# A fixed TensorE order for the projections of a hybrid DeltaNet and sparse-attention layer: chunk steps, transposes, projections and modulation interleaved

## The chip, the cores and the metric

The kernel runs on one core of a Trainium2 chip, in one launch. The metric is the device time of one execution in microseconds; a lower number is better. The kernel before took 3890.76 us (median of 3 runs, 3890.46 to 3893.05).

## What is computed

One inference step of one decoder layer, for a prompt of 2048 tokens (width 1024) and for 8 sampled tokens. Cut to what matters here:

```python
sh1, sc1, ga1, sh2, sc2, ga2 = split(silu(c) @ w_ada + b_ada, 6)       # modulation: 9 rows of c, w_ada is 1024 x 6144
h = rmsnorm(x, g_norm1) * (1 + sc1) + sh1
qkv, z, beta, a, aq, ak, av, iq, ik, iw = split(h @ w_in)               # w_in is 1024 x 3664
gq, gk, gv = silu(causal_conv4(qkv))                                   # then q and k are l2-normed
o_gdn = delta_rule_chunked(gq, gk, gv, decay, sigmoid(beta), s0)        # per chunk: (I + lower)^-1, then a state step
o_att = sparse_attn(rope(aq), rope(ak), av, rope(iq), rope(ik), iw)     # indexer picks 256 keys, then softmax
x = x + ga1 * (concat(rmsnorm(o_gdn) * silu(z), o_att) @ w_out)
h2 = rmsnorm(x, g_norm2) * (1 + sc2) + sh2
x = x + ga2 * ((silu(gate) * up) @ w_ffn_out)                           # gate, up = split(h2 @ w_ffn_in)
```

The outputs are the normed y of both, the new keys, values and index keys, the last rows before the convolution, and the new DeltaNet states.

## The kernel before

All matrix products keep fp32 precision. A large one is made of three matmuls (`mm3`, L157 to L162): operands are split into a high and a low part of the faster fp32r type, and high x high, high x low and low x high are added up in the same PSUM bank. So one product of a 128x128 block with 512 columns is three matmuls of 128x512, on lines L160, L161 and L162 of the profile.

The work is in two phases. Phase 1 (`phase1`) handles the prompt in four groups of 512 tokens; phase 2 does the attention of blocks 4 to 15 (128 queries each), the sampled rows, the output projection and the FFN.

**Phase 1** begins with the modulation. Parts 0 and 1 (shift and scale of the first norm) use the raw fp32 w_ada, which lies in borrowed buffers (L321); parts 2 to 5 are spread over the groups and go through `weights` like any other weight: load (L143), ScalarE cast to the high part (L144), VectorE subtraction for the low part (L145), and two matmuls per 128 rows against the split conditioning `cTs` (L176, L177).

For each group, `project(g)` norms the rows of x (ScalarE squares, VectorE scaling), transposes them on TensorE into hh and hl (8 x 4 transposes, L372), multiplies the 80 narrow columns (wsh, wsl), and then goes through seven column tiles of 512: three that feed the convolution, and z, aq, kv and iq. Each tile is 8 k steps x 12 matmuls into four PSUM banks ("d"); a group is 672 of them. Group 0 casts and splits w_in and stores the result in DRAM ("kept", L148); groups 1 to 3 load it back in 512 KB pieces (wi<-kept, L138, three buffers). `conv` (L637 to L652) evacuates a convolution tile (ScalarE L642, VectorE L646, L648, L651) and stores it in DRAM (cT_d). `narrow` makes decay and beta on 128x16 tiles (VectorE, L551 to L597). `tok` rotates aq, ak and iq (VectorE, L632 to L635) and transposes them (L676, L686, L722).

`chunks(g)` then runs the DeltaNet of the group: four chunks of 128 tokens, in two pairs. The two `chunk` generators of a pair alternate: load the chunk from cT_d (L814), transpose q, k, v (L829), norm them (VectorE L845, L847, L852), transpose again, decay matrix (L868 to L876), products k·k and q·k (L882). `inverse` inverts both chunks' four heads at once, as 8 dependent steps of 32 matmuls of 32x32 in four levels (E·D, L763; copy by ScalarE, L765; D part, L770; E part, L774; each followed by a VectorE copy under a mask, L771 and L775), and four larger steps (L781 to L804). `state` multiplies by the state, makes the new one and the chunk's output (L916 to L948). The inverse and the transposes use two PSUM banks ("g"), `state` and attention two ("s").

**What sets the order.** The scheduler of the language orders every engine's instructions from the program's order, priorities and its own estimate of time. On TensorE it puts whatever it believes ready in front: projection matmuls of group g+1 between chunk steps of group g, and also FFN matmuls of phase 2. An engine executes its list in that order.

Of the kernel before, what the change touches and what calls it, by code (L numbers as in the profile page):

```python
# [56 lines left out]
S2, S4, LATE = 8, 1044, 8000  # L57

# [51 lines left out]

class K:
    def __init__(self, tc, A, O, dbg=None, ngroups=NG, stages=9):
        self.tc, self.nc, self.A, self.O = tc, tc.nc, A, O
        self.dbg = dbg or {}
        self.ng = ngroups
        self.stages = stages
        self.biases, self.kept = {}, {}

# [39 lines left out]
    def mm3(self, out, wh, wl, xh, xl, start, stop, **kw):  # L158
        nc = self.nc
        nc.tensor.matmul(out, wh, xh, start=start, stop=False, **kw)  # L160
        nc.tensor.matmul(out, wh, xl, start=False, stop=False, **kw)  # L161
        nc.tensor.matmul(out, wl, xh, start=False, stop=stop, **kw)  # L162
# [10 lines left out]
    def mm_s(self, out, s, wh, wl, start, stop):  # L173

        n = s.shape[1]
        self.nc.tensor.matmul(out[:n], s, wh, start=start, stop=False)  # L176
        self.nc.tensor.matmul(out[:n], s, wl, start=False, stop=stop)  # L177
# [95 lines left out]
    def modulation(self):  # L273
# [26 lines left out]
        for k in range(KB):  # L300
            nc.tensor.transpose(pc[:, k * 9:k * 9 + 9], sc[:9, k * 128:(k + 1) * 128], self.id[:9, :9])
        self.cT = cp.tile([128, KB, 9], F32, name="cT")
        nc.scalar.activation(self.cT, pc[:, :72].rearrange("p (k n) -> p k n", k=KB), AF.Copy, scale=0.5)
        pt = self.ps.tile([128, 512], F32, name="d", tag="d", bufs=4)
        nc.tensor.transpose(pt[:, :113], vec[:113], self.id[:113, :113])
        nc.vector.tensor_copy(self.cv, pt[:, :113])
        self.cTs = self.stack(cp, self.cT, KB, 9, "cTs")
# [3 lines left out]
    def modulate(self, part):  # L311

        nc, A, p, wp = self.nc, self.A, self.p, self.wp
        for hf in range(2):
            c0 = part * 1024 + hf * 512
            b0 = part * 8 + hf * 4
            pm = self.ps.tile([128, 512], F32, name="d", tag="d", bufs=4)
            n = 9 if part < 2 else 42
            for k in range(KB):
                if part < 2:  # L320
                    nc.tensor.matmul(pm[:9], self.cT[:, k, :], self.ada[part][k][:, hf * 512:hf * 512 + 512], start=k == 0, stop=k == KB - 1)  # L321
# [3 lines left out]
            m9 = self.m("m9")[:n, :512]  # L325
            nc.scalar.copy(m9, pm[:n])
            pt = self.ps.tile([128, 512], F32, name="d", tag="d", bufs=4)
            for m in range(4):
                nc.tensor.transpose(pt[:, m * n:m * n + n], m9[:, m * 128:(m + 1) * 128], self.id[:n, :n])
            pv = pt[:, :4 * n].rearrange("p (m n) -> p m n", m=4)  # L330
            mod = self.mod[:, b0:b0 + 4, :]
            nc.vector.tensor_tensor(mod, pv[:, :, 0:9], self.cv[:, 16 + b0:20 + b0].unsqueeze(2).to_broadcast([128, 4, 9]), op=OP.add)
            if part >= 2:
                nc.vector.tensor_tensor(mod, mod, pv[:, :, 32:41], op=OP.add)
# [27 lines left out]
    def norm_T(self, xt, ms, Amul, Badd, hh, hl, ptag, pbufs):  # L362

        nc, nblk, xn = self.nc, 4, xt
        for t in range(0, nblk, 2):
            r = self.rnorm(ms[:, t:t + 2])
            for a in range(2):
                nc.vector.tensor_scalar(xn[:, t + a, :], xt[:, t + a, :], r[:, a:a + 1], None, op0=OP.mult)
        for k in range(KB):
            pt = self.ps.tile([128, 512], F32, name=ptag, tag=ptag, bufs=pbufs)  # L370
            for t in range(nblk):
                nc.tensor.transpose(pt[:, t * 128:(t + 1) * 128], xn[:, t, k * 128:(k + 1) * 128], self.id)  # L372
            h = self.p.tile([128, 512], F32, name="ca", tag="ca", bufs=2)
            nc.vector.tensor_scalar(h, pt, Amul[:, k, 0:1], Badd[:, k, 0:1], op0=OP.mult, op1=OP.add)
            nc.scalar.copy(hh[:, k, :], h)
            nc.vector.tensor_tensor(hl[:, k, :], h, hh[:, k, :].bitcast(F32), op=OP.subtract)

    def norm_T_s(self, pool, xs, ms, Amul, Badd, ptag, pbufs):
# [4 lines left out]
        for k in range(KB):  # L383
            nc.tensor.transpose(pt[:, k * NS:(k + 1) * NS], xn[:, k * 128:(k + 1) * 128], self.id[:NS, :NS])
# [6 lines left out]
    def phase1(self, es):  # L391
# [35 lines left out]
        self.modulate(0)  # L427
        self.modulate(1)
# [10 lines left out]
        self.ends()  # L439
# [22 lines left out]
    def project(self, g):  # L462
# [3 lines left out]
        xt = self.load_x(g) if g else self.x0  # L466
        hh = p.tile([128, KB, GT], F32R, name="hh", bufs=1)
        hl = p.tile([128, KB, GT], F32R, name="hl", bufs=1)
        ms = self.msq()
        for t in range(4):  # L470
            self.squares(ms[:, t], xt[:, t, :])
        self.norm_T(xt, ms, self.A1, B1, hh, hl, "d", 4)
        if samp:
# [3 lines left out]
            hs = self.norm_T_s(self.p1, xs, ms[:NS, 4:5], self.A1, B1, "d", 4)  # L477
# [3 lines left out]


        pd = self.ps.tile([128, 512], F32, name="d", tag="d", bufs=4)
        for k in range(KB):
# [1109 lines left out]
```

## Time and profile before

| | before |
|---|---|
| median of 3 runs | 3890.76 us (3890.46 to 3893.05) |
| profiled execution | 3895.36 us |
| its span | 3893.4 us |
| mean granted TensorE clock | 0.939 |
| TensorE / VectorE / ScalarE / GpSimd busy | 91% / 55% / 39% / 17% |
| idle before L774, behind VectorE's masked copy (54 to 1538 us) | 17.9 us in 16 waits |
| idle before L176, behind ScalarE's cast (54 to 1538 us) | 14.7 us in 20 waits |

A row of a timeline has the start, the length of the last record or of the group, the engine, the line, the operation, output and inputs, their shapes, the number of records, and in brackets the idle time before it with what ended that. fp32 matmuls leave two records each, fp32r matmuls one. In rows of windows the columns are the stretch, its length, the busy time of TensorE, its weight loads, VectorE, ScalarE and GpSimd with the number of instructions, then the granted TensorE clock (1.00 is full speed), the busy share of the DMA engines, and GB/s. A row of waits has the engine and line that waited, what it waited for, the total in us, how often, and the longest.

### The profile page before, as it was taken

How to read it: one execution, taken by the hardware profiler on the slowest of the kernel's cores; microseconds unless marked ns; L12 is line 12 of the kernel's file. 1: busy time of each engine (PE TensorE's matmuls, PEld its weight loads, DVE VectorE, ACT ScalarE, POOL GpSimd, SP SyncE). 2: the span in 40 equal slices, each digit the busy share in tenths (PEclk: the TensorE clock that was granted, in tenths of full speed). 3: DMA queues.
4: the chain of work that ended last, by engine and by line, in shares of the span. 5: the costliest groups of instructions: out<-in, count | busy, mean ns of one | idle time of the engine just before them, and what ended most of it. 6: DMA issues, size and time to landing. Idle time of an engine off the chain costs nothing.

```text
span 3893.4 us, 60837 instructions
## 1 busy us (share of the span) xinstructions
PE 3545.7 (91%) x22394; PEld 2733.7 (70%) x22394; DVE 2146.3 (55%) x4424; ACT 1506.7 (39%) x2909; POOL 651.1 (17%) x571
## 2 busy tenths in 40 slices
PE   8898888898898889999998999997899999889996
PEld 5767776686676568777766777675677787667774
DVE  3555544552664466766666563466766654444444
ACT  3333223232333333544445453355555533322232
POOL 1001000000000111121151111221112211412223
PEclk9898998898989799999999999998999999999998
DMA  6663453473456434455544333533333333422222
GB/s 236 215 236 118 152 191 127 132 245 133 147 175 206 126 111 136 114 165 168 152 139 153 111 115 101 155 109 103 105 107 103 91 107 98 136 99 81 81 84 67
DMA packets 391110, 528.61 MB, mean 136 GB/s; under 512 B 46804, under 2 KB 268153, under 8 KB 390794
## 3 DMA queue, kind: packets, MB, share of 16 engines
q1 hardware_dynamic: 390802, 524.63, 42.4%
q8 instruction: 178, 2.92, 0.3%
q14 instruction: 130, 1.06, 0.1%
HBM read 427.10 MB, written 116.36 MB: 140 GB/s over the span
## 4 chain that ended last, share of the span: by engine, by line
PE 52%; DVE 8%; DMA 6%; ACT 4%; issue 3%; POOL 2%; SPq 0%; ACTq 0%; DVEq 0%; POOLq 0%
PE d L160 13%; PE d L161 12%; PE d L162 12%; PE s L1333 2%; PE g L1401 2%; PE s L1376 2%; ACT bias L1228 2%; DVE wi L145 1%; PE g L1395 1%; ACT wi L144 1%; DMA wr<-in_w_out_dram 1%; DMA wr<-in_w_ffn_in_dram 1%; DMA ca<-oT_d 1%; PE g L176 1%; PE g L177 1%
## 5 line engine op out<-in xcount | busy, mean ns | idle before, releaser
L145 DVE TENSOR_TENSOR wi<-wr,wi 128x512 fp32r<-128x512 f32 x712 | 524.6, 742 | 784.6 <-ACT wi L144 775.0
L144 ACT CAST wi<-wr 128x512 fp32r<-128x512 f32 x712 | 437.8, 619 | 947.3 <-PE d L162 361.0
L160 PE MATMUL d<-hh,wi 128*128 128x512 f32 x1792 | 726.9, 407 | 6.6 <-ACT wi L144 4.3
L161 PE MATMUL d<-hl,wi 128*128 128x512 f32 x1792 | 709.3, 396 | 0.0
L162 PE MATMUL d<-hh,wi 128*128 128x512 f32 x1792 | 665.4, 397 | 0.0
L1450 POOL TENSOR_TENSOR xt<-xt,tm 128x512 f32<-128x512 f32 x224 | 326.9, 1476 | 516.0 <-DVE tm L1449 472.4
L160 PEld LDWEIGHTS d<-hh,wi 128*128 128x128 f32 x1792 | 339.1, 189 | 100.3 <-issue 13.7
L162 PEld LDWEIGHTS d<-hh,wi 128*128 128x128 f32 x1792 | 337.2, 189 | 83.2 <-issue 9.7
L161 PEld LDWEIGHTS d<-hl,wi 128*128 128x128 f32 x1792 | 339.3, 189 | 71.5 <-issue 7.6
L160 PE MATMUL d<-wi,hh 128*128 128x512 f32 x768 | 304.5, 418 | 25.4 <-DMA wi<-kept 11.4
L161 PE MATMUL d<-wi,hh 128*128 128x512 f32 x768 | 309.1, 403 | 0.4 <-DVE wi L145 0.4
L162 PE MATMUL d<-wi,hl 128*128 128x512 f32 x768 | 305.5, 402 | 0.0
L1526 POOL TENSOR_TENSOR al<-ca,ah 128x512 fp32r<-128x512 f32 x88 | 120.9, 1392 | 988.6 <-ACT ah L1525 987.6
L161 PE MATMUL d<-wi,ah 128*128 128x512 f32 x704 | 280.3, 401 | 0.5 <-DVE wi L145 0.5
L160 PE MATMUL d<-wi,ah 128*128 128x512 f32 x704 | 264.3, 412 | 17.5 <-ACT wi L144 5.5
L162 PE MATMUL d<-wi,al 128*128 128x512 f32 x704 | 274.7, 402 | 0.0
L1342 DVE SCALAR_TENSOR_TENSOR sc<-rl,iw,sc 128x512 f32<-128x512 f32 (+3 forms) x224 | 179.1, 800 | 87.3 <-ACT rl L1335 80.0
L1335 ACT ACTIVATE rl<-s 128x512 f32<-128x512 f32 (+3 forms) x288 | 149.6, 544 | 149.6 <-PE s L1333 108.9
L160 PEld LDWEIGHTS d<-wi,hh 128*128 128x128 f32 x768 | 148.8, 195 | 66.5 <-DMA wi<-kept 12.1
L1228 ACT ACTIVATE bias<-sc,sv 128x640 bf16<-128x640 f32 (+11 forms) x120 | 169.6, 1414 | 54.8 <-DVE sv L1226 27.3
L1449 DVE TENSOR_TENSOR tm<-d,row 128x512 f32<-128x512 f32 x224 | 150.5, 684 | 59.4 <-PE d L162 29.0
L1333 PE MATMUL s<-ik,iqT 128*128 128x512 f32 (+3 forms) x576 | 168.5, 397 | 11.1 <-ACT rl L1335 5.9
(521 smaller groups left out, 5548.3 us busy)
## 6 DMA issues: line engine op xcount, KB each, us to landing
wr<-in_w_ffn_in_dram SPq DMA_DIRECT2D x704, 128.0 KB
wi<-kept SPq DMA_DIRECT2D x168, 512.0 KB
wr<-in_w_ffn_out_dram SPq DMA_DIRECT2D x176, 256.0 KB
kept<-wi SPq DMA_DIRECT2D x56, 512.0 KB
xt<-in_x_prompt_dram SPq DMA_DIRECT2D x8, 2048.0 KB
wr<-in_w_ada_dram SPq DMA_DIRECT2D x64, 256.0 KB
wr<-in_w_out_dram SPq DMA_DIRECT2D x64, 256.0 KB
wr<-in_w_in_dram SPq DMA_DIRECT2D x56, 256.0 KB
```

The source lines that it names most:

```text
L144: nc.scalar.copy(w[:, 0], wr)
L145: nc.vector.tensor_tensor(w[:, 1], wr, w[:, 0].bitcast(F32), op=OP.subtract)
L160: nc.tensor.matmul(out, wh, xh, start=start, stop=False, **kw)
L161: nc.tensor.matmul(out, wh, xl, start=False, stop=False, **kw)
L162: nc.tensor.matmul(out, wl, xh, start=False, stop=stop, **kw)
L1228: nc.scalar.activation(c, s, AF.Sign, bias=t, accum_out=cnt)
L1333: nc.tensor.matmul(ps[:, :w], iq[:, h, :].bitcast(F32R), B["ikT"][c * 2 + a][:, :w].bitcast(F32R), start=a == 0, stop=a == 1)
L1335: nc.scalar.activation(r[:, :w], ps[:, :w], AF.Relu)
L1342: nc.vector.scalar_tensor_tensor(s, r[:, :w], iw, s, op0=OP.mult, op1=OP.add)
L1449: nc.vector.tensor_tensor(tm[:rows], pd[:rows], rw, op=OP.mult)
L1450: nc.gpsimd.tensor_tensor(xt, xt, tm[:rows], op=OP.add)
L1526: nc.gpsimd.tensor_tensor(al[b], a, ah[b].bitcast(F32), op=OP.subtract)
```

## The change

TensorE's order in phase 1 is written out. All TensorE calls go through a class `Ordered`; while it is switched on, each matmul or transpose gets a dependency without a semaphore on the one before, which ties the scheduler to the order in which the program makes them. (In the listing of the new order, all matmuls therefore have line L128 and all transposes L131; the tiles' names tell them apart.) It is on from the first projection to the end of the last one; what is left of the last pair of chunks and phase 2 are ordered by the scheduler as before.

The order itself comes from `weave`, which keeps a clock of TensorE time. Three generators run against it: the chain of chunk steps (`chain`), the rotations and their transposes (`toks`), and the projections (`projects`). Each yields the time that its step takes on TensorE and a pause until its next step may go; the first in this list whose pause is over is next. The constants are 0.225 us for a projection matmul, 0.44 for four transposes, 0.86 for four fp32 matmuls; the pauses are numbers such as 18 before the first chunk of a group, 11 for the norm of q and k, 0.8 and 0.6 within a level of the inverse.

With this go:

- The chunks of group g start when the convolution and narrow columns of g are done, and run beside the tiles z to iq of g and the projection of g+1.
- Transposes into hh, hl are made one k step at a time, two ahead, within the first column tile; the narrow matmuls come behind that tile. x of the next group is loaded, squared and scaled at the end of z.
- `modulate` uses raw fp32 weights for all six parts: no cast, no split, no `cTs`. The conditioning is padded to 32 columns, four k tiles are multiplied side by side into four 32-row strips of one PSUM bank, and eight small fp32 matmuls with four stacked identities (`f4`) fold the strips. The weights go to the two "row" buffers, two loads of 512 KB for each half of the k tiles.
- The new state is computed before the chunk's output, and the output's transposes come later.
- Hidden, narrow, rotation and modulation tiles move from the "d" banks to the two "s" banks; "d" holds only accumulators.
- Instructions of the chain on the other engines get a priority 3000 ahead.

```diff
+class Ordered:
+    def keep(self, made):
+        if self.on:
+            if self.last is not None:
+                self.tc.add_manual_dep(made.ins, self.last, mybir.DependencyInfo(mybir.DependencyClass.NoSync, mybir.DependencyReason.DATA),
+                                       reason="as written")
+            self.last = made.ins.name
+        return made
...
+    def weave(self, chain, *rest):
+        work = [dict(run=r, at=0.0, until=None) for r in (chain, *rest)]
+        while len(work) > 1:
+            for w in work:
+                if w["until"] is not None and w["until"]():
+                    w["at"], w["until"] = max(w["at"], self.now), None
+            able = [w for w in work if w["until"] is None]
+            first = min(w["at"] for w in able)
+            self.now = max(self.now, first)
+            w = next(w for w in able if w["at"] <= self.now)
+            if w["run"] is chain:
+                with self.tc.high_priority(offset=EARLY):
+                    said = next(chain, None)
+            else:
+                said = next(w["run"], None)
+            if said is None:
+                work.remove(w)
+            elif callable(said):
+                w["until"] = said
+            else:
+                self.now += said[0]
+                w["at"] = self.now + said[1]
...
-        self.project(0)
-        for g in range(self.ng):
-            self.chunks(g)
-            if g + 1 < self.ng:
-                if g:
-                    self.first_attn(g * 2 - 2)
-                self.project(g + 1)
-                self.modulate(g + 2)
-                if g == self.ng - 2:
-                    self.modulate(5)
+        self.pe.on = True
+        chain = self.chain()
+        self.weave(chain, self.toks(), self.projects())
+        self.pe.on = False
+        for _ in chain:
+            pass
         self.ends()
...
+            yield lambda: (g, "conv") in self.ready and (g, "narrow") in self.ready
+            yield 0, 18
...
-            for k in range(KB):
+            for a in range(2):
                 if part < 2:
-                    nc.tensor.matmul(pm[:9], self.cT[:, k, :], self.ada[part][k][:, hf * 512:hf * 512 + 512], start=k == 0, stop=k == KB - 1)
+                    w = [self.ada[part][a * 4 + k][:, hf * 512:hf * 512 + 512] for k in range(4)]
                 else:
-                    wh, wl = self.weights([A["w_ada"][0, k * 128:(k + 1) * 128, c0:c0 + 512]])
-                    self.mm_s(pm, self.cTs[:, k, :], wh, wl, k == 0, k == KB - 1)
+                    two = [p.tile([128, D], F32, name="row", tag="row", bufs=RB).rearrange("p (a c) -> p a c", a=2) for _ in range(2)]
+                    for j, t in enumerate(two):
+                        r0 = (a * 4 + j * 2) * 128
+                        nc.sync.dma_start(t, A["w_ada"][0, r0:r0 + 256, c0:c0 + 512].rearrange("(a p) c -> p a c", a=2))
+                    w = [two[k // 2][:, k % 2] for k in range(4)]
+                    yield 0, 4
+                pm = self.ps.tile([128, 512], F32, name="s", tag="s", bufs=2)
+                for k in range(4):
+                    self.pe.matmul(pm[k * 32:k * 32 + 32], self.cT[:, a * 4 + k, :], w[k], start=True, stop=True)
...
             Y = v8(t("Y")[:, :256])
             nc.scalar.copy(Y, py)
+            yield 0.5, 0.8
             pp = P()
...
                 for b in R:
-                    nc.tensor.matmul(pe[b, j, :], Y[b, j, :], E[b, j, :], start=True, stop=True)
+                    self.pe.matmul(pe[b, j, :], Y[b, j, :], E[b, j, :], start=True, stop=True)
             nc.vector.copy_predicated(E, mask(2 + 2 * lv), pe)
+            yield 1, 0.6
```

How TensorE's list changes is seen at two places. The first is an inverse beside a projection. Before, in the list of TensorE, at the second pair of the first group (g is the PSUM bank of the inverse; Dm holds D and E; smT are the narrow columns; d<-hh,wi is a projection matmul):

```order
L162 MATMUL d<-hh,wi 128x512
L763 MATMUL g<-Dm,E 32x32 x32
L538 MATMUL d<-cf,smT 128x80 x4
L770 MATMUL g<-Y,Dm 32x32 x32
L774 MATMUL g<-Dm,Y 32x32 x32
L763 MATMUL g<-Dm,E 32x32 x32
L770 MATMUL g<-Y,Dm 32x32 x32
```

And after, at the first pair of the second group (d<-wi,hh and d<-wi,hl are projection matmuls, s<-row,cT is the modulation on raw weights):

```order
L128 MATMUL d<-wi,hh 128x512 x2
L128 MATMUL d<-wi,hl 128x512
L128 MATMUL g<-Dm,E 32x32 x32
L128 MATMUL s<-row,cT 32x512 x4
L128 MATMUL g<-Y,Dm 32x32 x32
L128 MATMUL g<-Dm,Y 32x32 x32
L128 MATMUL d<-wi,hh 128x512 x2
L128 MATMUL d<-wi,hl 128x512
L128 MATMUL g<-Dm,E 32x32 x32
```

The steps of the inverse stood next to each other before; now projection or modulation matmuls stand between the levels and between E·D and its follower, while the D part and the E part of one level still follow each other directly.

The second place is the start of a pair of chunks beside the modulation. Before, in TensorE's list, at the second group's second pair (ct is the loaded chunk, decb, AT and kd belong to `state`, iqs are the rotated index queries, cTs the split conditioning):

```order
L927 MATMUL s<-decb,AT 128x128
L930 MATMUL s<-decb,kd 128x128 x4
L829 MATMUL g<-cf,ct 128x128 x8
L722 MATMUL d<-cf,iqs 128x128 x4
L176 MATMUL d<-wi,cTs 42x512
L177 MATMUL d<-wi,cTs 42x512
```

And after, at the start of the second group's first pair:

```order
L128 MATMUL d<-wi,hh 128x512 x2
L128 MATMUL d<-wi,hl 128x512
L128 MATMUL s<-row,cT 32x512 x4
L131 MATMUL g<-cf,ct 128x128 x24
L128 MATMUL d<-wi,hh 128x512 x2
```

The split modulation matmuls, which stood at the end of a group without projections beside them, are gone; four raw ones stand among projection matmuls. The 24 transposes of the two chunks, which came in pieces of 4 to 12, now follow one another.

More of the change, by code (lines that the diff above doesn't have):

```diff
@@ L1 @@
 import math
+from collections import deque
 from contextlib import ExitStack
@@ L117, in __init__ @@
         self.biases, self.kept = {}, {}
+        self.pe = Ordered(tc)
+        self.now, self.queue, self.ready, self.keep = 0.0, deque(), set(), {}
     def pool(self, es, name, bufs=1, space=None):
@@ new lines, in chain @@
+    def chain(self):
+        late = ()
+        for g in range(self.ng):
+            yield lambda: (g, "conv") in self.ready and (g, "narrow") in self.ready
+            yield 0, 18
+            for c in range(0, 4, 2):
+                k = [{}, {}]
+                for said in self.pair([self.chunk(g, c + a, k[a]) for a in range(2)], late):
+                    yield said
+                E = self.inv[(g * 2 + c // 2) % 2]
+                yield from self.inverse([k[a].pop("NT") for a in range(2)], (g * 2 + c // 2) % 2)
+                yield lambda: (g, "z") in self.ready
+                late = []
+                for a in range(2):
+                    yield from self.state(g, c + a, late, E=E[:, a * 4:a * 4 + 4, :].rearrange("p h e -> p (h e)"), **k[a])
+            if 0 < g < self.ng - 1:
+                for run in late:
+                    yield from run
+                late = ()
+                yield from self.first_attn(g * 2 - 2)
+        for run in late:
+            yield from run
@@ new lines, in pair, with toks @@
+    def pair(self, runs, late):
+        work = [[self.now, r] for r in (*runs, *late)]
+        while work:
+            w = min(work, key=lambda a: a[0])
+            if w[0] > self.now:
+                yield 0, w[0] - self.now
+            said = next(w[1], None)
+            if said is None:
+                work.remove(w)
+            else:
+                w[0] = self.now + said[0] + said[1]
+                yield said[0], 0
+    def toks(self):
+        while True:
+            yield lambda: self.queue or "end" in self.ready
+            if not self.queue:
+                return
+            yield from self.queue[0]
+            self.queue.popleft()
@@ new lines, in projects @@
+    def projects(self):
+        nxt = None
+        for g in range(self.ng):
+            rows, nxt = nxt, None
+            extra = iter(()) if not g else self.several(*((self.modulate(g + 1), self.modulate(5)) if g == self.ng - 1 else (self.modulate(g + 1),)))
+            run = self.project(g, rows)
+            while True:
+                said = next(run, None)
+                if said is None:
+                    break
+                if said == "mark":
+                    more = next(extra, None)
+                    if more is not None:
+                        yield more[0], 0
+                elif isinstance(said, list):
+                    nxt = said
+                else:
+                    yield said
+            for said in extra:
+                yield said[0], said[1]
+        yield lambda: not self.queue
+        self.ready.add("end")
@@ L441, in copy_pages, with several @@
+    def several(self, *runs):
+        for r in runs:
+            yield from r
     def copy_pages(self):
@@ L1302, in first_attn, with all @@
                  bias=one("dec", 512, BF), big=one("Dm"), rl=one("decb"), PT=one("Y"), oT=one("v"))
-        self.attn((i0, i0 + 1), B, False)
+        for i in (i0, i0 + 1):
+            yield from self.index(i, B, False)
+        if i0:
+            yield 0, 25
+        for i in (i0, i0 + 1):
+            yield from self.attend(i, B, self.biases.pop(i))
+    def all(self, run):
+        for _ in run:
+            pass
     def attn(self, blocks, B, general, then=None, part=None):
```

430 lines of the change are left out of this document (256 added, 174 removed).

## Prediction

> **What bounds the kernel now.** I read the page first, then a table of the span cut into stretches, then TensorE's waits in the part that the change touches, then single instructions there.
>
> ```profile
> span 3893.4 us, 60837 instructions
> PE 3545.7 (91%) x22394; PEld 2733.7 (70%) x22394; DVE 2146.3 (55%) x4424; ACT 1506.7 (39%) x2909; POOL 651.1 (17%) x571
> ```
>
> TensorE is busy for 91% of the span, so only its idle time, its slow clock and its own work can give anything. The cuts in the table are the transposes that begin each group's projection (54, 356, 689, 1020, 1460), and 1538, where TensorE starts the index matmuls of block 4. I use that last point as a marker: everything behind it is the second phase.
>
> ```profile
> 0.00:54.00 54.00, 40.01 (x122) 12.90 (x122) 15.66 (x31) 16.26 (x39) 8.88 (x25) 0.94 0.77 280
> 54.00:356.00 302.00, 270.58 (x2102) 217.73 (x2103) 150.55 (x360) 101.64 (x229) 13.31 (x14) 0.88 0.59 198
> 356.00:689.00 333.00, 291.52 (x3004) 235.49 (x3004) 172.92 (x406) 90.75 (x214) 21.44 (x21) 0.89 0.47 153
> 689.00:1020.00 331.00, 288.46 (x2988) 233.15 (x2987) 170.53 (x430) 95.28 (x230) 20.59 (x24) 0.91 0.50 166
> 1020.00:1460.00 440.00, 376.93 (x3970) 295.95 (x3968) 240.31 (x591) 150.62 (x342) 38.45 (x37) 0.88 0.47 153
> 1460.00:1538.00 78.00, 77.06 (x525) 65.31 (x525) 43.15 (x83) 25.12 (x43) 10.58 (x16) 0.93 0.42 136
> 1538.00:3893.00 2355.00, 2201.18 (x9692) 1673.16 (x9692) 1353.19 (x2528) 1026.97 (x1814) 537.86 (x434) 0.97 0.38 115
> ```
>
> From 54 to 1460 TensorE looks 87 to 90% busy, but at a clock of 0.88 to 0.91; afterwards the clock is 0.97. "Busy" thus hides slow matmuls. To see what the work would cost undisturbed, I price it from start to start of neighbouring records at full clock. (Rows: start, length; x64 records of 32x32 are 32 matmuls.)
>
> ```profile
> 404.74 0.39 PE L162 MATMUL d<-hh,wi 128*128 128x512 f32 x1
> ...
> 406.10 0.39 PE L162 MATMUL d<-hh,wi 128*128 128x512 f32 x1
> 406.42 0.75 PE L763 MATMUL g<-Dm,E 32*32 32x32 f32 x64
> 407.10 0.50 PE L538 MATMUL d<-cf,smT 80*128 80x80 f32 x4
> 407.64 0.75 PE L770 MATMUL g<-Y,Dm 32*32 32x32 f32 x64
> 410.49 0.54 PE L774 MATMUL g<-Dm,Y 32*32 32x32 f32 x39 [2.10 <-DVE Dm L771]
> ...
> 414.39 1.39 PE L770 MATMUL g<-Y,Dm 32*32 32x32 f32 x64 [1.91 <-DVE Dm L775]
> 419.00 1.08 PE L774 MATMUL g<-Dm,Y 32*32 32x32 f32 x64 [3.21 <-DVE Dm L771]
> ```
> ```profile
> 508.35 0.60 PE L829 MATMUL g<-cf,ct 128*128 128x128 f32 x4
> 508.78 0.60 PE L946 MATMUL s<-cf,qe 128*128 128x128 f32 x4
> ```
> ```profile
> 652.68 0.39 PE L927 MATMUL s<-decb,AT 128*128 128x128 f32 x2
> ...
> 653.80 0.39 PE L926 MATMUL s<-S,qeT 128*128 128x128 f32 x2
> ```
> ```profile
> 27.02 3.60 PE L321 MATMUL d<-hl,cT 128*9 128x512 f32 x8
> 30.46 1.02 PE L321 MATMUL d<-qk,cT 128*9 128x512 f32 x2
> ```
>
> A projection matmul costs 1.36/6 = 0.227 us, an inverse step of 32 matmuls 0.68, a transpose 0.43/4 = 0.107, a 128-wide fp32 matmul 1.12/5 = 0.224, a 512-wide fp32 one 3.44/4 = 0.86. Counting TensorE's instructions in the order of before up to the marker: 3108 projection matmuls 705.5, transposes 111, inverse 89, state and attention in fp32 90, modulation 59.5, the rest (narrow columns, sample rows, the kq products, index; the same in both kernels) 85 by the same prices. That is 1139 of the 1538 us. The missing 399 us are what the change can attack: 21 in the start, 9 in the last stretch and 368 in the four middle stretches, whose demand is 1038 of 1406.
>
> The rows from 406 show where they come from. Eight dependent inverse steps stand together with no projection matmul between; each waits 2 to 3 us for VectorE, whose queue is full of convolution and narrow work, and then TensorE runs at half clock (L770 takes 1.39 for 0.68 worth of work). The waits in the region agree, spread over many hand-offs (total us, times, longest):
>
> ```profile
> PE g L774 <- DVE Dm L771: 17.9, 16, 3.2
> PE d L176 <- ACT wi L144: 14.7, 20, 1.4
> PE d L160 <- DMA wi<-kept: 13.0, 14, 2.9
> PE g L882 <- DVE AT L888: 12.2, 6, 3.1
> PE g L829 <- DVE qk L852: 7.2, 7, 1.9
> PE d L160 <- DVE ca L374: 7.1, 3, 4.2
> PE g L794 <- DVE low L791: 5.3, 5, 2.2
> ```
>
> **The change, part by part.**
>
> *Demand.* In the new order the marker is TensorE's row 3029. Before it stand 2880 projection-shaped matmuls, 228 fewer: those were FFN matmuls that the scheduler had used as filler, and they now come later. That takes 51.8 us out before the marker and adds 52 behind it, at full price, since I can't count on a gap there. Modulation: parts 2 to 5 lose their 128 split matmuls, 64 ScalarE casts and 64 VectorE subtractions (off TensorE's path except for L176's 14.7 us). All six parts now take 96 fp32 matmuls of 32 columns, four side by side, 96 x 0.86/4 = 21, and 96 fold matmuls of a quarter of 0.224, 5 to 6. I take 26.4.
>
> ```profile
> 2192.23 1.92 PE L1148 MATMUL s<-s,s 128*32 128x512 f32 x14
> ```
>
> This row, seven such matmuls in neighbouring column groups, gives 1.92/7 = 0.27 each, 5 us more; four that ran one by one would be 62 more, but nothing here is near that. Demand before the marker: 1139 - 52 - 33 - 2 (a few transposes) = 1053 (start 9, woven part 974, tail 70).
>
> *Start.* Parts 0 and 1 need 8.4 MB of w_ada; at the first stretch's 280 GB/s that is 30 us, and x with its norm follows. TensorE's own 33 us shrink to 9, so the load now bounds.
>
> ```profile
> 60.54 0.39 PE L160 MATMUL d<-hh,wi 128*128 128x512 f32 x1
> ```
>
> The first projection matmul came at 60.5; I take 48 (the eight hidden transposes up front and the narrow matmuls, 43 to 60 before, now stand behind it or between). Loss 38, from 30 to 45.
>
> *Woven part.* Each chain step now has projection matmuls on both sides, some 9 (2.04 us) per inverse level. What stays open, term by term:
>
> (a) Within a level, E·Y is followed directly by Y·E, which waits for VectorE's copy out of the same bank, 31 times.
>
> ```profile
> 1315.92 0.96 PE L774 MATMUL g<-Dm,Y 32*32 32x32 f32 x52 [0.55 <-DVE Dm L771]
> ```
>
> The clean wait is 0.55; the mean of L774's row is 17.9/16 = 1.12. Middle 0.83: 26 (17 to 35). (b) The tail of the inverse, L794, mean 1.06, once in each of 8 pairs: 8 (4 to 17). (c) Transposes in a row (24, then 32) through two "g" banks and the kq products: three bursts per pair, L829's mean 1.03: 25 (10 to 46). (d) 14 state steps at about 1 us: 14 (7 to 31). (e) Group starts 4 x 2.4 (L160 behind ca) and 28 changes of accumulator at 0.5, an estimate below the 0.55 above: 24 (10 to 45). (f) Weight reloads: the 13.0 stays; the 512 KB w_ada loads get two k tiles of time (24 x 0.227 = 5.4 us), so a few us for SP's queue, past which they are now moved: 20 (0 to 41). (g) Clock, below: 25 (0 to 60). (h) The chain's start.
>
> ```profile
> 498.19 0.69 DVE L651 SCALAR_TENSOR_TENSOR cth<-cth,ca 128x512 f32<-128x512 f32 x1 [1.49 <-ACT cth L650]
> ```
> ```profile
> 503.72 0.80 SPq L814 DMA_DIRECT2D ct<-cT_d  x2
> ```
>
> From the last convolution to the chunk's transposes at 508.35 it took 10 us, of which the copy to DRAM and back is the most; the order allows 18 from the point where VectorE is only given that work. I take 6 us short, four times: 24 (8 to 38). Sum 166, from 56 to 313.
>
> *Clock.* The order decides it as much as the waits do:
>
> ```profile
> 622.00:626.00 4.00, 4.00 (x43) 2.76 (x41) 1.73 (x6) 1.83 (x4) 0.00 (x0) 1.00 0.39 118
> 630.00:634.00 4.00, 1.81 (x108) 1.42 (x98) 1.79 (x7) 1.81 (x5) 0.00 (x0) 1.00 0.23 78
> 634.00:638.00 4.00, 3.29 (x105) 2.80 (x100) 2.24 (x8) 1.90 (x5) 1.25 (x4) 0.60 0.37 135
> ```
> ```profile
> 632.25 0.63 PE L722 MATMUL d<-cf,iqs 128*128 128x128 f32 x4 [1.89 <-DVE iqs L718]
> ```
>
> The last projection matmul here ends before 626. The longest gap after it is 1.89 us, and still the clock falls to 0.60 at 634: a stretch of small matmuls with short gaps was enough. The new order still has such bursts of transposes, three a pair; I charge 8 pairs x 3 us, about one half-clock burst each (25); the ends are 0, if all stay like 622 to 626, and 60, if three bursts of 2.5 us in each pair run at half clock. The Trainium skill (TensorE: Matmul & The Clock Gate, section HAM oscillation — how this bites in real kernels) gives the rule that there be no idle gap of TensorE over some 3.4 us. By it these bursts would keep full clock, (g) would be 0 and the time 25 us less; the rows here disagree.
>
> *Tail.* The last pair of group 3 stays as the scheduler has it: 12 (9 before).
>
> *At no cost.* The order adds no instruction or semaphore. The chain's higher priority on the other engines, the kept gc and beta, and the early norm of the next group lie under the projections (VectorE is busy half of the time there); uncovered, a norm would cost its group start's 4.2 again.
>
> Sum: 1053 + 38 + 166 + 12 = 1269 to the marker instead of 1538; + 2355 + 52 = 3676 span. The profiled run lasted 3895.36, 2 us over its span, and 4.6 over the median of the runs (3890.76): 3678 as profiled, 3673 as a median.
>
> **The rivals.**
>
> *Fuller cover* (0.15). The weave's pauses are right and the clock stays up: (a) 17, (e) 12, (f) 13, (h) 12, others none, 54 instead of 166: 3561. For it: 622 to 626 above, full clock with chain steps between. Against: the bursts.
>
> *Clock stays down* (0.08). The chain's small matmuls, some 23 us a pair (inverse 11, transposes 6, kq and state the rest), run at half clock throughout as at L770 in 414: 8 x 23 = 184 instead of 25: 3832. Against: about 40% of such a stretch are projection matmuls now.
>
> *The loss stays in proportion* (0.10), that is, the change doesn't do what it says: only TensorE is ordered, VectorE's queue still makes the steps late. Loss 368/1038 of 974 = 345 instead of 166: 3852.
>
> *Slower* (0.08). A fixed order can't step around a late operand. If the inverse steps, 92 of them, each find VectorE as late as the longest L771 row, 3.2 us, because convolutions of the next group stand in its queue, every projection matmul behind stands still too: 92 x 3.2 = 294 for (a) and (b), 260 more: 3933. It decides from 2.7 us a step (217 us to no change, plus the 34 in the sum, over 92). For it: 410 to 419, in just that mixture of work. Against: chain work now has priority on VectorE. The Trainium skill (TensorE: Matmul & The Clock Gate, Step-by-step: what each phase is for) says that matmuls stay in program order; the waits above, behind which ready projection matmuls stood, agree.
>
> **How the numbers follow.** The forecast, 0.56, is 3673; its own range is 3600 to 3780. All lower ends together give 3673 - 110 - 8 = 3555, all upper ends 3673 + 147 + 7 = 3827. The range 3540 to 3840 holds it, the fuller cover and the clock rival, 0.79, and a little of the proportional one. About 0.2% (8 us) is what a measurement of this kernel can tell from no change. Faster 0.56 + 0.15 + 0.08 + 0.10 = 0.89; slower 0.08; between the last two cases there is a coincidence near 3890, 0.03.
>
> **What would show it.** Right: index of block 4 starts near 1269; stretches of the groups of 280 to 300 us at clock 0.93 or more; L771's waits near 0.8, about 31 times; no L176 line; the second phase about 2407. Wrong: waits of 2 to 3 us before inverse steps (slower, proportion); a clock of 0.9 with short waits (clock); a first projection matmul at 60; a second phase that gives more than 52 back.

## The result and the profile after

| | before | after |
|---|---|---|
| median | 3890.61 us (4 runs, 3890.26 to 3893.05) | 3788.62 us (4 runs, 3781.41 to 3792.82) |
| span of the profiled execution | 3893.4 us | 3779.5 us |
| mean granted TensorE clock | 0.939 | 0.964 |

The ratio is 0.9735, with a 95% interval of 0.9718 to 0.9751: 102 us faster, where 218 were forecast. The direction was right and the time lies within the range, but less than half of the gain came.

The table of stretches of the kernel after, cut where each group's hidden transposes begin (52.5, 388, 668, 968.7), where the rows of `ffn(0)` begin (1285.3) and at the marker, the index of block 4 (1388):

```profile
0.00:52.50 52.50, 33.00 (x145) 15.76 (x145) 9.60 (x21) 15.90 (x41) 8.50 (x24) 0.77 0.78 284
52.50:388.00 335.50, 300.09 (x3132) 238.16 (x3132) 188.20 (x435) 104.70 (x232) 17.41 (x22) 0.95 0.53 178
388.00:668.00 280.00, 253.76 (x2874) 198.34 (x2872) 144.80 (x343) 79.33 (x193) 14.02 (x17) 0.98 0.55 182
668.00:968.70 300.70, 273.47 (x2978) 215.65 (x2976) 159.47 (x408) 86.68 (x215) 17.07 (x24) 0.96 0.56 182
968.70:1285.30 316.60, 289.93 (x2732) 225.19 (x2731) 181.02 (x489) 105.23 (x254) 12.86 (x15) 0.95 0.54 178
1285.30:1388.00 102.70, 81.16 (x758) 66.49 (x752) 51.20 (x101) 36.80 (x77) 27.33 (x30) 0.90 0.47 154
1388.00:3779.50 2391.50, 2244.37 (x9936) 1716.09 (x9936) 1383.24 (x2561) 1043.38 (x1845) 535.18 (x438) 0.97 0.38 115
```

The clock of the woven stretches is 0.95 to 0.98 now. In the records the clock is 0.5 or 1, in pieces of 3.4 us or a multiple of it; between 54 and 1460 it stood at 0.5 for 314 us before, and between 52.5 and 1285.3 for 96 us after. The waits of TensorE there have changed as well:

```profile
PE g L128 <- DVE Dm L957: 19.8, 30, 1.6
PE g L128 <- issue: 14.6, 16, 2.4
PE d L128 <- DVE cth L833: 11.4, 7, 3.8
PE d L128 <- DMA wi<-kept: 6.8, 6, 1.8
PE s L131 <- DVE iqs L910: 6.4, 8, 1.1
PE g L128 <- DVE AT L1080: 4.3, 2, 2.4
...
PE g L131 <- DMA ct<-cT_d: 1.0, 1, 1.0
```

The wait between the D part and the E part of a level is there 30 times (L957), 0.66 us each, a little under the 0.83 forecast. Of the wait for a chunk's data at the chain's start, forecast at 24 us, 1 us is left (the last line).

**Where the forecast and the span differ.** The forecast was 3676 us of span, the profile has 3779.5:

| part | forecast | after | difference |
|---|---|---|---|
| start | 47 | 52.5 | +5 |
| woven part | 974 + 166 = 1140 | 1232.8 | +93 |
| tail up to the marker | 82 | 102.7 | +21 |
| second phase | 2407 | 2391.5 | -15.5 |

I added up the woven part from TensorE's whole timeline, record by record. The idle times that the profile puts in brackets are 113 us. The clock is halved for 92 us outside these waits, of which half, 46 us, is lost (a projection matmul takes 0.47 us there to the start of the next record, and 0.25 at full clock). The instructions at their prices are 988 (14 more than forecast, see below). That leaves 86 us that are none of these; I call them the rest. The forecast had 141 for waits, 25 for the clock, and nothing for the rest. The same sum for the stretch 54 to 1460 of the kernel before gives 1038 of work, 177 of waits, 121 of clock (242 us at half clock outside the waits) and 70 of the rest. **So waits and clock together came out near the forecast, 159 us against 166 (the waits 28 lower, the clock 21 higher), and the rest, which the forecast left out, did not shrink: it grew by 16.** The experiments are on what it is.

### The profile page after: what moved, and what is told of

Read it like the earlier page. It is cut to its first block, busy times and chain, and to the rows that moved or that the text cites. A ratio compares the mean times of both kernels' runs of the same rounds, so it can differ in the third digit from the quotient of the medians.

```text
span 3779.5 us, 60914 instructions
## 1 busy us (share of the span) xinstructions
PE 3475.8 (92%) x22538; PEld 2675.7 (71%) x22538; DVE 2117.5 (56%) x4352; ACT 1472.0 (39%) x2856; POOL 632.4 (17%) x570
## 4 chain that ended last, share of the span: by engine, by line
PE 60%; DVE 12%; DMA 6%; issue 5%; ACT 4%; POOL 1%; SPq 1%; ACTq 0%; DVEq 0%; POOLq 0%
PE d L128 43%; PE s L128 7%; PE g L128 6%; PE g L131 2%; DMA wr<-in_w_ffn_in_dram 2%; ACT bias L1433 1%; DVE wi L170 1%; DMA wr<-in_w_ffn_out_dram 1%; DVE tm L1669 1%; ACT wi L169 1%; PE s L131 1%; DVE sc L1556 1%; DMA wi<-kept 1%; DVE big L1592 1%; DVE ca L820 1%
## 5 line engine op out<-in xcount | busy, mean ns | idle before, releaser
L128 PE MATMUL d<-hh,wi 128*128 128x512 f32 x3584 | 1216.2, 403 | 12.6 <-ACT wi L169 6.9
L170 DVE TENSOR_TENSOR wi<-wr,wi 128x512 fp32r<-128x512 f32 x648 | 490.5, 761 | 675.3 <-ACT wi L169 670.9
L128 PEld LDWEIGHTS d<-hh,wi 128*128 128x128 f32 x3584 | 674.2, 189 | 184.5 <-issue 17.7
L169 ACT CAST wi<-wr 128x512 fp32r<-128x512 f32 x648 | 398.7, 619 | 844.1 <-PE d L128 285.2
L128 PE MATMUL d<-hl,wi 128*128 128x512 f32 x1792 | 708.0, 395 | 1.4 <-DVE hl L416 1.3
L128 PE MATMUL d<-wi,hh 128*128 128x512 f32 x1536 | 516.4, 418 | 31.6 <-DVE cth L833 11.4
L128 PE MATMUL d<-wi,ah 128*128 128x512 f32 x1408 | 461.1, 408 | 16.7 <-DVE tm L1669 6.3
L128 PEld LDWEIGHTS d<-hl,wi 128*128 128x128 f32 x1792 | 339.1, 189 | 73.3 <-issue 7.8
L128 PEld LDWEIGHTS d<-wi,hh 128*128 128x128 f32 x1536 | 283.9, 195 | 106.0 <-DVE cth L833 14.5
L128 PEld LDWEIGHTS d<-wi,ah 128*128 128x128 f32 x1408 | 261.4, 190 | 104.0 <-DVE tm L1669 11.6
L128 PE MATMUL d<-wi,hl 128*128 128x512 f32 x768 | 307.2, 403 | 0.0
L128 PE MATMUL d<-wi,al 128*128 128x512 f32 x704 | 274.2, 401 | 0.0
L128 PEld LDWEIGHTS d<-wi,hl 128*128 128x128 f32 x768 | 149.4, 195 | 34.2 <-issue 0.7
L128 PE MATMUL s<-ik,iqT 128*128 128x512 f32 (+3 forms) x576 | 163.3, 387 | 9.8 <-ACT rl L1549 6.5
L128 PEld LDWEIGHTS d<-wi,al 128*128 128x128 f32 x704 | 133.1, 190 | 31.7 <-issue 1.9
L128 PE MATMUL g<-PT,V 128*128 128x256 f32 x504 | 136.7, 393 | 17.5 <-ACT PT L1615 17.5
```

What stands on the lines that cost most here:

```text
L128: return self.keep(self.engine.matmul(*a, **k))
L169: nc.scalar.copy(w[:, 0], wr)
L170: nc.vector.tensor_tensor(w[:, 1], wr, w[:, 0].bitcast(F32), op=OP.subtract)
```

## The experiments

The first theory was that each change of TensorE between projection matmuls and the chain's small fp32 ones costs time by itself (the rest). The rival was that changes are free and only late operands count (the waits).

**e1, the order switched off.**

```diff
-        self.pe.on = True
+        self.pe.on = False
```

> The changed kernel with the fixed order switched off: the program makes the same instructions in the same order with the same priorities, and the scheduler may place TensorE's as before. If the fixed order itself gives the gain: about 3850 to 3880 (only the cheaper modulation, 15 to 40 us, is left of 102). If the new program order, the priorities and the bank moves give it: within 10 us of 3789.

3838.89 us, ratio to before 0.9862 (0.9843 to 0.9882). So 50 of the 102 us come from the fixed order, and the remaining 52 from the other parts of the change, more than I expected of them. Its stretch 54 to 1400:

```profile
54.00:1400.00 1346.00, 1209.01 (x12318) 978.80 (x12318) 691.08 (x1713) 394.55 (x942) 86.60 (x94) 0.90 0.52 170
```

The clock is 0.90 there, about as before the change, not 0.95 to 0.98. By the same sum half clock costs 104 us in this stretch beside the waits (136), against 46 and 113 in the woven part with the order, whose work is 53 us less: what the order gives is above all the clock.

**e2, the modulation alone**, put into the kernel before.

```diff
-            for k in range(KB):
...
-                    self.mm_s(pm, self.cTs[:, k, :], wh, wl, k == 0, k == KB - 1)
+            for a in range(2):
...
+                for k in range(4):
+                    nc.tensor.matmul(pm[k * 32:k * 32 + 32], self.cT[:, a * 4 + k, :], w[k], start=True, stop=True)
```

> The kernel before with only the modulation on raw weights (all parts, four k tiles side by side, folded), everything else as before. If the modulation's casts and its 14.7 + 6.3 us of waits mattered: 3890 less 13 us of TensorE work less up to 21 us of waits, about 3855 to 3875. If they were hidden, or its loads through two buffers now wait in turn: 3885 to 3895.

3880.06 us, ratio 0.9967 (0.9955 to 0.998): 13 us, between the two expectations. The waits for the cast and the split are gone but for 0.8 us, yet a new one stands in their place, that for the raw weights in their two buffers:

```profile
PE d L329 <- DMA row<-in_w_ada_dram: 12.9, 13, 2.3
```

**e3 and e4, more pieces and more cover.** e3 cuts each of the three 32x32 steps of a level in two (the last of the three is shown); e4 puts one projection triple between the D part and the E part.

```diff
...
                 for b in R:
                     self.pe.matmul(pe[b, j, :], Y[b, j, :], E[b, j, :], start=True, stop=True)
+                if j == 3:
+                    yield 0.34, 0.01
```
```diff
             nc.vector.copy_predicated(D, mask(1 + 2 * lv), pd)
+            yield 0.68, 0.01
...
-            yield 1, 0.6
+            yield 0.68, 0.6
```

> The changed kernel with each of the twelve steps of the four levels of an inverse cut in two halves of 16 matmuls, one triple of projection matmuls or other work put between: about 96 pieces more, no work more. Theory 1, each change between kinds of matmul costs 0.25 to 0.3 us without any wait: 24 to 29 us slower, about 3815. Theory 2, changes are free and only late operands cost: within 8 us of 3789, or faster, since each step gets more cover.

> The changed kernel with one triple of projection matmuls between the D part and the E part of each level, where TensorE waits 20.5 us in 32 waits for VectorE's masked copy. Theory 1 (a change of kind costs): 18 us of waits go, 32 more changes cost about 9, so about 9 us faster, 3780. Theory 2 (only late operands cost): 18 to 20 us faster, about 3770.

e3: 3773.63 us (0.9681, 0.9659 to 0.9703), e4: 3753.70 us (0.9648, 0.963 to 0.9667). Both are faster than the changed kernel, e4 by 35 us, more than either theory gave. In e4 the wait behind L957 shrinks to this:

```profile
PE g L128 <- DVE Dm L957: 3.8, 6, 2.0
```

Taken alone this speaks for the rival. e4's stretch up to the end of the projections (53.8 to 1249.9) is 37 us shorter, of which 22 are waits, 10 slow clock and 5 work that now lies behind it; so the covered wait brought more than its own 16 us.

But e3's timeline (54.4 to 1253.5), added up in the same way, has 26 us less of waits and 7 us more of the rest for its pieces. (Here and below each record of the trace has the price of its shape. So reckoned the work of the woven part is 977 us, not 988, and the rest is 97 us in the changed kernel and 76 in the kernel before.) And e3 does not get faster by covering the wait behind the masked copy, which is still there:

```profile
PE g L128 <- DVE Dm L961: 21.8, 28, 1.6
```

What goes in e3 is above all the 15 us of waits with no releaser (issue), of which it has none; e13 is on these. So both theories could be true.

**e5, four pieces** instead of e3's two, at the same three places.

```diff
...
+                if j in (1, 3, 5):
+                    yield 0.17, 0.01
```

> The changed kernel with each of the twelve 32x32 steps of an inverse cut in four pieces of 8 matmuls with a triple of projection matmuls between (e3 had two pieces, 3774). About 192 pieces more than e3. If each piece costs the 0.1 us that e3's trace shows on each side of it plus 0.1 for the slower first projection matmul: 3774 + 45 to 58, about 3825. If changes of kind cost nothing and cover is all: 3774 or less.

3838.84 us (0.9865, 0.984 to 0.989), 65 us slower than e3 and slower than either expectation. The rival can't explain it by late operands: the waits in its stretch 54 to 1257 are the same as e3's (86 and 87 us) while the rest grows from 104 to 144. But the chain is also longer here, and its end reaches further into the second phase, so this is no clean price.

**e6, half of the folds**, the two halves of the modulation added by VectorE:

```diff
-                got.append(self.m("m9")[:, :512])
-                nc.scalar.copy(got[a], pm)
+                if a == 0:
+                    got.append(self.m("m9")[:, :512])
+                    nc.scalar.copy(got[0], pm)
+                else:
+                    nc.vector.tensor_tensor(got[0], got[0], pm, op=OP.add)
...
-                for a in range(2):
-                    self.pe.matmul(pt[:, m * 32:m * 32 + 32], got[a][:, m * 128:(m + 1) * 128], self.f4, start=a == 0, stop=a == 1)
+                self.pe.matmul(pt[:, m * 32:m * 32 + 32], got[0][:, m * 128:(m + 1) * 128], self.f4, start=True, stop=True)
```

> The changed kernel with the two halves of the modulation added up by VectorE, so that four fold matmuls do instead of eight, 48 fewer in all. At the 0.24 us each that the changed kernel's trace shows: 11 us faster than 3789, about 3778. At the 0.056 that the prediction used: 3 us, not to be told from 3789.

3780.79 us (3763.99 to 3785.11), ratio 0.9707 (0.9673 to 0.9741): 8 us below the changed kernel, with intervals that overlap. The price itself can be read; in the changed kernel's timeline eight fold matmuls (16 records) take 1.90 us from start to start, 0.24 each:

```profile
1271.02 1.97 PE L128 MATMUL s<-cf,m 128*128 128x32 f32 x16
1272.92 0.75 PE L128 MATMUL g<-Y,Dm 32*32 32x32 f32 x64
```

**e7, no priority for the chain.**

```diff
-MM, TP, F4, EARLY = 0.225, 0.44, 0.86, 3000
+MM, TP, F4, EARLY = 0.225, 0.44, 0.86, 0
```

> The changed kernel with no priority for the chain on the other engines (EARLY 0 instead of 3000); TensorE's order is the same. If the fixed order lives from VectorE and ScalarE taking chain work first: each of some 100 inverse steps finds VectorE 0.5 to 3 us late, 3840 to 3950. If the scheduler's own order of the other engines, which follows from TensorE's, does as well: within 10 us of 3789.

3789.81 us (0.9738, 0.9713 to 0.9763): no difference. VectorE and ScalarE don't need to be told; with TensorE's order given, the scheduler finds an order for them that does as well. The prediction counted on that priority against the slower rival; it turns out not to be what kept VectorE in time.

**e8, transposes spread:** e4 with a pause behind each of the six sets of four transposes of a chunk (one is shown).

```diff
-        yield TP, 0
+        yield TP, 0.6
```

> e4 (3754) with a pause of 0.6 after each set of transposes of a chunk, so that the runs of 24 and 32 transposes through two PSUM banks are broken by projection triples. If cover decides: the waits of about 12 us and the 0.25 us by which sets follow each other late (about 14 us) go, 15 to 25 us faster than e4, about 3735. If changes of kind cost 0.3 us a piece: some 40 pieces more, 12 us back, about 3745 to 3752.

3743.82 us (0.9634, 0.9599 to 0.9669), 10 us below e4; with runs that lie 12 and 23 us apart and intervals that overlap this is likely, not certain.

**e9, fewer pieces without the chain:** in group 0 the sample rows' matmuls stand once behind the four triples of a k step instead of behind each.

```diff
...
-                    if samp:
-                        for part, w in enumerate((wh, wl)):
+                for m in range(4 * samp):
+                    s = slice(m * 128, (m + 1) * 128)
+                    for part, w in enumerate((wh, wl)):
...
```

> The changed kernel with the sample rows' matmuls of group 0's three convolution tiles put together once per k step (24 pieces) instead of behind every projection triple (96 pieces); same matmuls, no chain runs beside them. In the changed kernel's trace the first projection matmul behind such a piece takes 0.083 us longer. If a change of kind costs that: 72 x 0.083 = 6 us less between the first projection and group 0's narrow matmuls, and 6 us less in all, 3783. If the longer first record is only how the profile divides time: no difference in that stretch.

3791.95 us (0.9737, 0.972 to 0.9755): no difference. In the trace the time from the first hidden transposes to the last convolution triple falls from 105.5 (52.53 to 158.01) to 103.1 us (52.88 to 156.01), of which 1.3 is one wait. So a change to these matmuls of the same fp32r kind costs next to nothing, under 0.02 us, and the longer first record behind them is mostly how the profile divides the time.

**e12, e13, e14: pieces by themselves.** e12 leaves out the chain, that is the DeltaNet of the prompt and the attention of blocks 0 to 3, and stores zeros for them, so its outputs are not the layer's. e13 and e14 add to e12 448 steps of 32 matmuls of 32x32 on constants, which wait for no other engine; e13 has one step to a piece and a projection triple behind it, e14 two steps and two triples.

```diff
...
+        for _ in range(448):
+            for _ in range(1):
+                for j in range(8):
+                    for b in R:
+                        self.pe.matmul(v[b, j, :], self.id[b, 0:32], self.id[b, 0:32], start=True, stop=True)
+            yield 0.68 * 1, 0.68 * 1 - 0.01
...
```

This is e13; e14 has 224 for 448 and 2 for 1.

> The changed kernel without the chain: no DeltaNet chunks and no attention of blocks 0 to 3 (zeros are stored in their place), so that only projections, rotations, narrow columns and modulation stand in the fixed order. The chain's own work up to the marker is about 270 us at isolated prices; waits and slow clock there are 131. If the 114 us that neither waits nor the clock nor the prices explain belong to the projections' stream anyway: 3789 - 270 - 131 = 3388. If they come with the chain's pieces: 3274.

> e12 with 448 steps of 32 matmuls of 32x32 on constants between the projection triples, one step to a piece, behind the first convolution; they wait for no other engine and nobody reads them but once. 448 x 0.68 = 305 us of work. If a piece costs 0.3 us besides its work: e12 + 305 + 134, and e13 - e14 = 224 x 0.3 = 67 us. If changes of kind are free: e12 + 305, and no difference from e14.

> The same 448 steps with two to a piece, 224 pieces, each followed by two projection triples. If a piece costs 0.3 us: 67 us faster than e13; if changes of kind are free: equal to it within 10 us.

3361.07, 3929.59 and 3942.65 us (ratios to before 0.8637, 1.008 and 1.0137, each within 0.004). The projections' stretch of each:

```profile
72.00:910.50 838.50, 781.30 (x3698) 612.76 (x3697) 344.21 (x889) 242.03 (x583) 6.02 (x10) 0.97 0.70 231
```
```profile
70.00:1474.50 1404.50, 1233.90 (x32369) 903.72 (x32369) 349.75 (x890) 242.71 (x583) 6.02 (x10) 0.95 0.43 141
```
```profile
70.00:1459.00 1389.00, 1167.04 (x32373) 902.40 (x32371) 348.35 (x891) 242.90 (x583) 5.98 (x10) 0.95 0.44 142
```

e12 lies between its two expectations. Both count 131 us of waits and slow clock in the changed kernel and 114 of the rest, with only 18 for the clock; with the 46 above it is 159 and 86. And both took the waits and the slow clock for gone, but 57 and 22 us of them are still there in this stretch. The rest is 33 us in it, against 97 with the chain: about a third of the rest belongs to the projections' stream anyway, two thirds come with the chain.

e13 lies 129 us above the higher of its expectations. 448 steps lengthen the stretch by 566 us, 1.26 us a step, though a step costs 0.68 by itself: 305 are work, 111 waits, 39 slow clock and 111 the rest. The rest is 144 us in e13 and 76 in e14. So from e13 to e14 224 pieces go and 68 us with them: **0.30 us a piece**, where 0.3 was expected. Where nothing waits, it can be read from the starts, in e13 and then in e14:

```profile
309.63 0.75 PE L128 MATMUL g<-cf 32*32 32x32 f32 x64
310.32 0.73 PE L128 MATMUL d<-wi,hh 128*128 128x512 f32 x2
310.88 0.40 PE L128 MATMUL d<-wi,hl 128*128 128x512 f32 x1
311.21 0.57 PE L128 MATMUL g<-cf 32*32 32x32 f32 x43
```
```profile
235.75 1.29 PE L128 MATMUL g<-cf 32*32 32x32 f32 x128
236.97 0.73 PE L128 MATMUL d<-wi,hh 128*128 128x512 f32 x2
237.53 0.39 PE L128 MATMUL d<-wi,hl 128*128 128x512 f32 x1
237.76 0.62 PE L128 MATMUL d<-wi,hh 128*128 128x512 f32 x2
238.23 0.40 PE L128 MATMUL d<-wi,hl 128*128 128x512 f32 x1
238.55 1.63 PE L128 MATMUL g<-cf 32*32 32x32 f32 x128
```

One step and one triple take 1.58 us in e13, so two of each 3.16; in e14 two steps and two triples take 2.80, which is 0.36 less for one piece less. The projection matmul before a change takes 0.33 us to the next start and the one behind it 0.34, instead of 0.23; the remainder lies at the end of the run of small matmuls.

Yet e14's stretch is only 15.5 us shorter, and the whole kernel is not faster: it is 13 us slower than e13, with intervals that just touch, so neither of e14's expectations came. What takes the place is idle time of TensorE with no releaser, in the midst of runs of small matmuls. From the two timelines, e13 and then e14, with the totals:

```profile
402.56 0.26 PE L128 MATMUL g<-cf 32*32 32x32 f32 x6
404.18 0.89 PE L128 MATMUL g<-cf 32*32 32x32 f32 x58 [1.36 <-issue]
```
```profile
403.88 0.21 PE L128 MATMUL g<-cf 32*32 32x32 f32 x1
406.04 1.27 PE L128 MATMUL g<-cf 32*32 32x32 f32 x127 [1.95 <-issue]
```
```profile
PE g L128 <- issue: 125.7, 151, 3.7
```
```profile
PE g L128 <- issue: 167.3, 160, 4.0
```

A run of 32 or 64 small matmuls stops in the middle; with TensorE's other waits of this kind it is 137 us in e13 and 189 in e14, none in e12. They are waits for instructions, as the DMA records of the same traces show: of the 162 such stops in e13, 160 end 1.2 to 1.65 us after a packet of the instruction queue has landed, where 9% of moments taken at random in that stretch and none of TensorE's 24 other waits do. In the changed kernel it is all 17 of its stops, against 4% of random moments and 3 of 138 other waits. e3 and e5, whose runs are 16 and 8 small matmuls long, have no such stop.

Both theories of the start are thus half right: the price of a piece is real, and a longer run, which has fewer pieces, can pay it back by waiting for its instructions.

**e10 and e11, the best of them.** e10 is e8 with e6's folds; e11 adds e9's batching and longer pauses.

```diff
-                yield 0, 0.5 if b else 4
+                yield 0, 1.6 if b else 4
...
-        yield 0, 8
+        yield 0, 11
...
-        yield 0.3, 1.2
+        yield 0.3, 1.9
...
-        yield 0.4, 1.2
+        yield 0.4, 1.9
```

> e8 (3744) with e6's halved folds: 48 x 0.24 = 11 us at most, 8 measured on the changed kernel; 3733 to 3737 if the two add up, 3744 if TensorE's order had other work waiting there anyway.

> e10 with e9's batching and three longer pauses in the weave (index queries 0.5 to 1.6, output transposes 8 to 11, the inverse's last steps 1.2 to 1.9), against the waits L910, r4y and L979 of e4's trace, 18 us together. If late operands are the rest: 10 to 20 us below e10, 3715 to 3728. If the pauses only move the wait to the next step of the chain, whose length grows: within 6 us of e10.

3737.85 us (ratio 0.9608, 0.9585 to 0.963) and 3733.77 us (0.9584, 0.9571 to 0.9598). e10 lies 6 us below e8, about what e6 gave; the pauses of e11 bring no difference that its spread can tell. e11 is the fastest measured: 157 us below the kernel before, 55 below the changed one.

## Why the prediction was wrong in size

- **"The missing 399 us are what the change can attack."** This step failed. It took the distance between isolated prices and the span for waits and slow clock, and then forecast 166 us of both. But 70 of the 368 us in the middle stretches were the rest even before, and 86 are there after. The sum had no term for it. With the 14 us of demand it is more than the whole 93 us by which the woven part came out longer; waits and clock together gave 7 back. As the records show it (97 us), the rest has several parts, all estimates: about 27 us lie at the edges of 94 pieces of small matmuls between projections (32x32, 64x64 and the modulation's 32-row strips), some 0.29 each. About 27 lie at the waits: a bracket begins when the last matmul's record ends, some 0.18 us after the next one could have started, and there are 155 of them. About 12 lie between transposes in a row. The remaining 30 or so are spread and stay open. Before the change there were 42 such pieces between projections, so the order made more of them and could not lower this part.
- **Waits** (terms a to f and h): 141 forecast, 113 measured. (a) 26 against 19.8; e4 shows that covering this wait is worth more than its length, since 35 us went with it. (h) 24 against 1: the 18 us before a chunk suffice. (f) 20 against 6.8. The third largest wait before the change is missing from the prediction's list; 12.6 us of it are one wait at 110 us, for the narrow columns of group 0:

```profile
PE d L579 <- DVE gt L573: 14.3, 2, 12.6
```

With the narrow matmuls behind a tile 0.5 us of it is left; in e1, without the order, it is 13.1.

- **Clock** (g): 25 against 46, a term that was too small. That small matmuls with short gaps halve the clock was right, and e1 shows that it is the larger part of the order's gain. But the forecast charged one burst of about 3 us a pair, and the clock stood at 0.5 for 12 us a pair, of which more than half outside the waits (53 of 92 us) fell on projection matmuls. The clock rival and the proportional rival did not come, but the proportional one was not far: the woven part's loss is 245 us over its work, between the 166 forecast and that rival's 345, though not through the late vector work on which it rested.
- **Demand:** fold matmuls were priced by their columns, 0.056 us, but take 0.24, nearly a 128-column matmul's 0.224: with 128 rows and columns of stationary operand the few moving columns bring no discount here. 56 of the 96 folds lie in the woven part; that is 10 of the 14 us.
- **Tail:** 12 us of loss forecast, 31 measured, since I gave it only the loss of the stretch before. There, FFN matmuls lay beside the last chunks. Now TensorE waits for the rows of `ffn(0)` and for the index queries:

```profile
PE d L131 <- DVE xt L405: 12.9, 1, 12.9
PE s L128 <- DMA iqT<-iqT_d: 3.0, 1, 3.0
```

- **Second phase:** 52 us for the 228 displaced FFN matmuls, 36.5 measured; some may have found gaps, which was not looked into.
- **Slower** did not come: the longest wait for VectorE's copy is 1.6 us, 3.2 before, and its threshold was 2.7 in the mean.
- **Of the gain that did come**, 50 us are the fixed order (e1), about 13 the modulation (e2, in the kernel before). If these add up, the other 39 are the remaining parts of the change together, without the order: the program's own sequence, the bank moves and the priorities, of which the last give nothing with the order in place (e7). They were not taken apart further.

## What to carry to other kernels

Before a gap between "work at isolated prices" and the span is called removable, add up the timeline: bracketed waits, slow clock, and what remains. Another order can win the first two; what remains follows the number of pieces and of waits, and here it grew. Count the pieces of an interleaving and give each a price, and cover the shortest regular wait first: one triple of projection matmuls between two dependent steps was worth more here than the rest of the fine tuning together. A fixed order pays by keeping the clock up even more than by filling waits.

## What was not expected of the hardware

- A step of 32 fp32 matmuls of 32x32 costs 0.68 us in isolation, but 1.26 us each when 448 of them stand among projection matmuls (e13): 0.25 us is the rest, above all the change of kind, 0.25 us is waiting, above all for instructions, and 0.09 is slow clock. The instruction queue moves much more in these kernels, here in e12 and e13 (packets, MB, share):

```profile
q8 instruction: 113, 1.85, 0.2%
```
```profile
q8 instruction: 337, 5.52, 0.6%
```

That is 3.67 MB more for 14336 matmuls, 256 bytes each. That TensorE waits for its instructions in such runs is shown by the moments at which its stops end (e13). The Trainium skill (Runtime: NRT & Kernel Launch, section Instruction fetch mechanics) says that the fetch is hidden by the pace at which instructions are issued; for such short matmuls it is not, with 137 us of stops in e13.
- The price of a change goes with the size of the small matmuls, not with fp32. Behind 32x32 matmuls the first projection matmul takes 0.34 us, and the last small one 0.12 instead of 0.01. Behind the fp32 transposes of 128x128 the first projection matmul takes 0.315, but the last transpose gives way after 0.03 us instead of 0.11, so that the change costs 0.01. The fp32r matmuls of the sample rows cost under 0.02 us a piece (e9).
- VectorE and ScalarE kept up without any priority for the chain (e7, 3789.81 against 3788.62).
